# Differential attention: three query tiles transposed behind their scores, alternating with the next head's scores; bias copies in two lots

## The chip, the cores and the metric

One core of one Trainium2 chip. The metric is device time in microseconds of one execution; the kernel is run several times and the median is given. A core has a tensor engine (PE) with a weight loader (PEld), a vector engine (DVE), a scalar engine (ACT), GpSimd (POOL) and a queue that issues the DMAs here (SP). PE writes its products to PSUM, eight banks of 128 x 512 fp32; DVE and ACT read them there.

## The reference

A two-layer encoder on two sequences of 512 and 256 tokens (768 together), width 1024. Cut to what matters here:

```python
# layer 0
h = x @ w_in                                   # u | v | q | k | v_attn
out_a = gelu(u) * (W_s[g] @ layer_norm(gelu(v)) + b[g])
s = q_row @ k_win + rpb[:, row_off][:, :, col_off]   # 8 heads x 64, neighbourhood window
out_b = softmax(s) @ v_win
x = layer_norm(ALPHA * x + concat(out_a, out_b) @ w_out)
x = layer_norm(ALPHA * x + square(relu(x @ w1)) @ w2)
# layer 1: differential attention, 8 heads, two maps of 64, values of 128
s = q @ k - slope[h] * abs(q_pos - k_pos)      # both maps
p = softmax(s)
o = (p[0] - lam * p[1]) @ v
x = layer_norm(ALPHA * x + (rms_norm(o, g) * (1 - lam_init)) @ w_out)
x = layer_norm(ALPHA * x + square(relu(x @ w1)) @ w2)
```

## The kernel before

**Numbers.** Every fp32 operand of a product is split into a high part (rounded to the PE's fp32r form, on ACT: `xh`, `wh`, a "CAST") and a low part (the rest, a subtraction on DVE: `xl`, `wl`, a "TENSOR_TENSOR"). `mm3` issues three matmuls for each product: high x high, high x low, low x high (L128, L129, L130). So every weight that comes in by DMA (`raw`) passes ACT and DVE before PE can use it (`weights`, L137 on), and every PSUM result that becomes an operand passes `split` (L132).

**Tiles and stages.** The 768 tokens are six query tiles of 128: t = 0 to 3 are the long sequence, t = 4 and 5 the short one. Names of tiles end in the stage: V is the first projection (the gate's v, six PSUM banks at once, eight steps of k), U the gate's u and the first head's q and k, N0 to N7 the neighbourhood heads, O0 the output projection, F and G the MLP, D0 to D7 the differential heads of layer 1, O1 its output projection, then F and G again.

**What sets the order.** PE and SP run in the order in which the code is written. DVE, ACT and POOL are ordered by the framework's scheduler, which goes by readiness and by priorities (`high_priority`). PSUM has two groups of banks: five "pa" (scores, transposes, value products) and three "ps" (projections). A tile of a group can be written only after the last reader of the tile that held its bank is done, and banks are handed out in turn.

**Stage V and what follows.** For k = 0 the first weight comes in two halves; `between=ask` puts the two DMAs of x (columns 0 to 383, 384 to 767) behind the first half on SP, and the splits of the weight halves and of the two column spans stand behind them in the code. Before the data is there PE runs nine matmuls of ones (`warm(9)`). After V's last matmul, stand in the code: `na_copies` (twelve DMAs on SP that lay the positional bias out in DRAM scratch: eight of 8x16x512, four of 8x32x512; no other stage touches them before a head's `na_load` reads them back), the weight loads of the first three jobs (`per[:3]`: q0, k0, u0, u1), gate vectors, the spatial weights `wsb` and `bsb`, the next weight (u2), the gate's gelu and norm (`gate_norm`: gelu L191, squares L195, norms L198 and L199) with the DMAs that lay the gated rows out in chunk order (`vc`), `warm(14)` (28 matmuls in the profile), and then stage U. `gate_norm` reads V's six PSUM banks: four "pa" and two "ps".

**Heads.** `attention` makes three lists for a head: S (scores of tile t, two half scores of 128x512 for t < 4 in layer 1, then a softmax on DVE and ACT: a fused add, minimum and accumulate L339, exp L341, reciprocal L342, the combination of the two maps L1278 and L1279), T (four PE transposes of 128x128 of a tile's p, L373, then `split` into `pt` or, for t = 4 and 5 with two transposes, into `sp`), and V (value products of the long sequence from `pt`, then of the short one from `sp`). `pipeline` strings the heads together: with lag 2 a head is S0 S1, then T4 T5 and V of the head before (`carry`), then S2 T0 S3 T1 S4 T2 S5 T3. `weave` puts the fill matmuls (projections of the next head, output projection) between them by their costs; of the first `held` items only twelve fill items may stand between. In layer 1 the RMS norm of the head before (`pend`) is run at t == 2.

In the last neighbourhood head the four second-half weights of O0 (`last`, `wo0[4..7]`) are loaded, cast on ACT and subtracted on DVE.

Of the kernel before, what the change touches and what calls it, by code (L numbers as in the profile page):

```python
# [72 lines left out]
class Trunk:  # L73
# [44 lines left out]
    def stat(self, w=1):  # L118
        return self.small.tile([P, w], F32, tag=f"st{w}", name=self.uid("st"), bufs={1: 24, 2: 4, 6: 4}[w])

# [15 lines left out]
    def weights(self, src, pool=None, spare=False, parts=1, between=None):  # L136

        nc = self.nc
        raw = self.wpool.tile([P, D], F32, tag="raw", name=self.uid("raw"), bufs=3)
        if pool is None:  # L140
            hi, lo = [self.wpool.tile([P, D], F32R, tag="w", name=self.uid(n), bufs=8) for n in ("wh", "wl")]
        else:
            hi, lo = [pool.tile([P, D], F32R, tag="w2", name=self.uid(n)) for n in ("wh", "wl")]
        for i in range(parts):
            cs = slice(i * D // parts, (i + 1) * D // parts)
            nc.sync.dma_start(raw[:, cs], src[:, cs])
            if between and i == 0:
                between()
            nc.scalar.copy(hi[:, cs], raw[:, cs])
            (nc.gpsimd if spare else nc.vector).tensor_tensor(lo[:, cs], raw[:, cs], hi[:, cs].bitcast(F32), op=ALU.subtract)  # L150
        return hi, lo
# [199 lines left out]
    def attention(self, pl, prob, values, emit):  # L351
# [12 lines left out]
        def tr(t):  # L364
            def f():
# [8 lines left out]
                if t >= 4 or not self.near:  # L374
                    c = self.tok(t - base)
                    if t < 4:
                        hi, lo = [x.rearrange("p (k c) -> p k c", c=NP) for x in (hi, lo)]
                    with self.tc.high_priority(200):
                        self.split(ps[:, :n * P].rearrange("p (k c) -> p k c", c=P), hi[:, k0:k0 + n, c], lo[:, k0:k0 + n, c])
                    return  # L380

                steps = [offs[k0 + j] + (t - q0[k0 + j]) * P for j in range(n)]
                for i, (lo_j, hi_j) in enumerate(self.runs(steps)):
                    d = steps[lo_j + 1] - steps[lo_j] if hi_j - lo_j > 1 else P
                    src = ps[:, lo_j * P:hi_j * P].rearrange("p (k c) -> p k c", c=P)
                    dst = [bass.AP(tensor=x.tensor, offset=x.offset + steps[lo_j],
                                   ap=[list(x.ap[0]), [d, hi_j - lo_j], [1, P]]) for x in (hi, lo)]
                    with self.tc.high_priority(200):
                        self.split(src, dst[0], dst[1])
            return f  # L390
# [127 lines left out]
    def pipeline(self, mains, fills, wait, lag=2):  # L518


        carry = []
        for u, (S, T, V) in enumerate(mains):
            main = S[:lag] + carry
            held = len(main)
            for t in range(lag, TT):
                main += [S[t], T[t - lag]]
            carry = T[TT - lag:] + V
            if u == len(mains) - 1:
                main += [(wait, fn) for _, fn in T[TT - lag:]]
                carry = V  # L530
            weave(main, fills[u], held, 12, 1.08 if self.near else 1.04, (1500 if self.near else 3600) if u else 0,
                  lambda fn: self.scored >= getattr(fn, "after", 0))
        run(carry)

# [23 lines left out]
    def mix0(self, ahead):  # L558
# [29 lines left out]
        def mixed(g, sample):  # L588
# [7 lines left out]
            for j in range(n):  # L596
# [12 lines left out]
                [vjob(1)], [qjob(3), kjob(3)], [(oA[0], oA[1][:6])], [(oA[0], oA[1][6:])]]  # L609
        last = self.lazy(lambda: [self.weights(a["wo0"][4 + j]) for j in range(4)])  # L610
        fills = self.fillers(per)
        self.ph = "V"
        self.near, self.first, self.count, self.pw = True, (0, 0, 1, 2), (2, 3, 3, 2), 512
        self.warm(9)
        vps = [self.bank("pa" if t < 4 else "ps") for t in range(TT)]
        for k in range(NK):
            if k == 3:
                scratch, stores = self.na_rows(pl)
            if k == 6:
                for dst, src in stores:  # L620
                    nc.sync.dma_start(dst, src)
            xr = pl.tile([P, NT], F32, tag="h", name=self.uid("xr"))
            def ask():
                for c, d in SPANS if k == 0 else [(0, NT)]:
                    nc.sync.dma_start(xr[:, c:d], a["xt"][k][:, c:d])
            if k:
                ask()
            if k % 2 == 0:
                ws = self.weights(a["wv0"][k // 2], parts=1 if k else 2, between=None if k else ask)
            for c, d in SPANS:  # L630
                self.split(xr[:, c:d], self.xH[:, k, c:d], self.xL[:, k, c:d])
            wh, wl = [w[:, (k % 2) * 512:(k % 2) * 512 + 512] for w in ws]
            for t in range(TT):
                cs = self.tok(t)
                self.mm3(vps[t], self.xH[:, k, cs], self.xL[:, k, cs], wh, wl, k == 0, k == NK - 1)
        self.na_copies(scratch)
        self.key_lows(pl)
        for js in per[:3]:
            for ws, _ in js:
                ws()  # L640
        gates = pl.tile([P, 3, 512], F32, tag="h", name="gates")
        gg, gb = gates[:, 0, :], gates[:, 1, :]
# [5 lines left out]
        for ws, _ in per[3]:  # L648
            ws()
        vg, vc = [[pl.tile([P, 3, 512], F32, tag="h", name=f"{n}{h}") for h in range(2)] for n in ("vg", "vc")]  # L650
        gated = self.gate_norm(vps, [vg[i // 3][:, i % 3, :] for i in range(TT)],
# [11 lines left out]
        self.raws = [self.na_load(pl, tables, h) for h in range(1)]  # L663
        self.warm(14)
        self.ph = "U"
# [119 lines left out]

    def na_copies(self, scratch):


        for s in range(2):
            w, rows, rl = BLK[s], ROWS[s], ROWLEN[s]  # L790
            base, sc, step = scratch[s]
            for r in range(rows):
                self.nc.sync.dma_start(
                    bass.AP(tensor=sc.tensor, offset=sc.offset + r * w * step,
                            ap=[[P * step + w, NHEAD], [step + 1, w], [1, rows * rl]]),
                    bass.AP(tensor=base.tensor, offset=base.offset + (rows - 1 - r) * rl,
                            ap=[[RPB_ROWS[s] * rl, NHEAD], [0, w], [1, rows * rl]]))

# [449 lines left out]
    def mix1(self, ahead):  # L1248
# [5 lines left out]
        def unit(h):  # L1254
            self.cost_s, self.cost_r, self.cost_x, self.cost_t = 1300, 0.68, 0, 176

            def prob(t):
# [5 lines left out]
                w, c0 = c * P, 384 - P * t if t < 4 else 1024 - P * (t - 4)  # L1263
                if t == 2:
                    while pend:
# [70 lines left out]
        left = self.side("m1l", "left", dict(h=8))  # L1336
        right = self.side("m1r", "right", dict(v=2, p=6, pt=2, sp=2, tb=1, kl=1))
        pl = self.both(left, right)
# [11 lines left out]
        self.after_norm(lead)  # L1350
        self.pipeline([unit(h) for h in range(8)], fills, 2535)
        while pend:
# [116 lines left out]
```

## Time and profile before

| what | value |
|---|---|
| median of 3 runs | 1692.05 us (1691.17 to 1694.19) |
| the profiled execution, own time | 1689.46 us |
| its span in the profile | 1687.7 us |
| mean granted PE clock | 0.991 |
| DMA | 210.93 MB, mean 125 GB/s |
| first transposes of stage N wait (116.14 us) | 2.07 us for ACT's softmax |

A row of a timeline gives start, duration, engine, line, operation, written tile <- read tiles, shapes, count, and in brackets how long the engine was idle before it and who released it. A row of groups gives the line, engine, operation and count, then busy us and mean ns, then the idle time before. The granted clock is the share of full speed that PE had; 0.50 is half.

### The profile page before, as it was taken

Reading aid. Unit: us, or ns where it says so; the run is one execution under the profiler, and the core shown is the slowest. Engines: PE = TensorE matmul, PEld = TensorE weight load, DVE = VectorE, ACT = ScalarE, POOL = GpSimd, SP = SyncE. Lnnn points to the kernel's source line nnn. Section 1 sums busy time; section 2 is a strip of 40 time slices with the busy share of each in tenths; the row PEclk is TensorE's granted clock in tenths of the full one; section 3 lists DMA queues with packets and bytes.
Section 4 is the critical chain, followed back from the end, with each engine's and each line's share of the span. In section 5 each row is a group of like instructions: output and inputs, shape, how many; then the busy total and the mean of one; then the engine's idle time right before and its main releaser. Section 6 shows DMA issues by size and latency. Waiting matters only on the chain.

```text
span 1687.7 us, 23443 instructions
## 1 busy us (share of the span) xinstructions
PE 1633.7 (97%) x8926; PEld 1479.3 (88%) x8926; DVE 1226.9 (73%) x2117; ACT 933.7 (55%) x1698; POOL 45.5 (3%) x44
## 2 busy tenths in 40 slices
PE   8999998999999999999999999998999999999998
PEld 7889986899999888888988898886899999788886
DVE  3648778986766786887667676687987665786876
ACT  3546775466555544452667576775465566544442
POOL 0100000100000000001100000001100000000001
PEclk9999999999999999999999999999999999999999
DMA  7622212154355745461110111111154444745441
GB/s 246 207 96 69 69 57 76 51 198 149 140 174 186 266 141 176 145 206 61 51 50 26 50 51 38 38 38 50 51 198 173 174 167 150 265 143 183 149 165 75
DMA packets 113521, 210.93 MB, mean 125 GB/s; under 512 B 19824, under 2 KB 74352, under 8 KB 113408
## 3 DMA queue, kind: packets, MB, share of 16 engines
q1 hardware_dynamic: 113408, 209.43, 36.6%
q8 instruction: 70, 1.15, 0.3%
q14 instruction: 43, 0.35, 0.1%
HBM read 162.95 MB, written 49.08 MB: 126 GB/s over the span
## 4 chain that ended last, share of the span: by engine, by line
PE 73%; ACT 10%; DVE 9%; DMA 4%; issue 2%; SPq 1%; POOL 0%; DVEq 0%; POOLq 0%; ACTq 0%
PE psG L130 5%; PE psG L129 5%; PE psG L128 5%; PE psD L128 4%; PE psD L129 4%; PE psD L130 4%; PE psF L128 3%; PE psF L129 3%; PE psF L130 3%; PE paG L130 3%; PE paG L128 3%; PE paG L129 3%; PE paF L130 3%; PE paF L128 3%; PE paF L129 3%; DMA rwF<-in_ff_dram 2%
## 5 line engine op out<-in xcount | busy, mean ns | idle before, releaser
L128 PE MATMUL psG<-whG,hqG 128*128 128x512 f32 x336 | 131.4, 391 | 3.7 <-ACT hqG L133 3.7
L130 PE MATMUL psG<-whG,hqG 128*128 128x512 f32 x336 | 131.6, 392 | 0.5 <-DVE hqG L134 0.5
L129 PE MATMUL psG<-wlG,hqG 128*128 128x512 f32 x336 | 131.2, 391 | 0.0
L134 DVE TENSOR_TENSOR wlF<-rwF,whF 128x1024 fp32r<-128x1024 f32 x82 | 100.2, 1223 | 36.1 <-PE psF L129 31.3
L133 ACT CAST whF<-rwF 128x1024 fp32r<-128x1024 f32 (+1 forms) x110 | 102.8, 936 | 25.0 <-PE psF L129 23.2
L130 PE MATMUL paF<-xh,wlF 128*128 128x384 f32 x344 | 115.7, 336 | 0.0
L128 PE MATMUL paF<-xh,whF 128*128 128x384 f32 x344 | 115.4, 336 | 0.0
L129 PE MATMUL paF<-xl,whF 128*128 128x384 f32 x344 | 115.3, 335 | 0.0
L134 DVE TENSOR_TENSOR hqG<-hiG,hqG 128x768 fp32r<-128x768 f32 x106 | 100.4, 952 | 14.4 <-ACT hqG L133 14.4
L133 ACT CAST hqG<-hiG 128x768 fp32r<-128x768 f32 x106 | 87.6, 832 | 34.7 <-PE psG L130 17.9
L128 PE MATMUL psF<-xhO,whF 128*128 128x384 f32 x312 | 105.8, 339 | 0.6 <-DVE ctF L1047 0.4
L129 PE MATMUL psF<-xlO,whF 128*128 128x384 f32 x312 | 105.0, 337 | 0.0
L130 PE MATMUL psF<-xhO,wlF 128*128 128x384 f32 x312 | 104.8, 336 | 0.0
L128 PE MATMUL paG<-whG,hqG 128*128 128x512 f32 x252 | 98.0, 389 | 0.0
L129 PE MATMUL paG<-wlG,hqG 128*128 128x512 f32 x252 | 98.0, 389 | 0.0
L130 PE MATMUL paG<-whG,hqG 128*128 128x512 f32 x252 | 98.0, 389 | 0.0
L128 PE MATMUL psD<-xh,whD 128*128 128x384 f32 (+1 forms) x280 | 92.1, 329 | 0.0
L129 PE MATMUL psD<-xl,whD 128*128 128x384 f32 (+1 forms) x280 | 90.0, 322 | 0.0
L130 PE MATMUL psD<-xh,wlD 128*128 128x384 f32 (+1 forms) x280 | 90.0, 321 | 0.0
L341 ACT ACTIVATE pD<-pD,stD 128x512 f32<-128x512 f32 (+1 forms) x96 | 62.3, 649 | 32.4 <-DVE stD L339 32.2
L128 PEld LDWEIGHTS psG<-whG,hqG 128*128 128x128 f32 x336 | 63.5, 189 | 17.4 <-ACT hqG L133 4.3
L1005 ACT ACTIVATE ctF<-ctF 128x384 f32<-128x384 f32 x64 | 33.7, 526 | 81.2 <-DVE ctF L1047 80.6
(430 smaller groups left out, 4841.4 us busy)
## 6 DMA issues: line engine op xcount, KB each, us to landing
hiG<-hd SPq DMA_DIRECT2D x106, 384.0 KB
hd<-hsF SPq DMA_DIRECT2D x24, 1344.0 KB
rwF<-in_ff_dram SPq DMA_DIRECT2D x28, 1024.0 KB
gzG<-in_ff_dram SPq DMA_DIRECT2D x28, 512.0 KB
rawD<-in_wf_dram SPq DMA_DIRECT2D x16, 512.0 KB
rawG<-in_ff_dram SPq DMA_DIRECT2D x14, 512.0 KB
gyG<-in_ff_dram SPq DMA_DIRECT2D x14, 512.0 KB
hd<-hsO SPq DMA_DIRECT2D x4, 1344.0 KB
```

Source lines behind the costliest of these rows:

```text
L128: mm(ps, lh, rh, start=start, stop=False, **kw)
L129: mm(ps, lh, rl, start=False, stop=False, **kw)
L130: mm(ps, ll, rh, start=False, stop=stop, **kw)
L133: self.nc.scalar.copy(hi, src)
L134: self.nc.vector.tensor_sub(lo, src, hi.bitcast(F32))
L341: nc.scalar.activation(p, p, AF.Exp, bias=mn, scale=-1.0, accum_out=sm)
L1005: nc.scalar.activation(x, src, AF.Relu)
```

## The change

- `pipeline` gets a lag of 3 in layer 1: a head begins S0 T3' S1 T4' S2 T5' (the primes are tiles of the head before), then V of the head before, then S3 T0 S4 T1 S5 T2. The last head ends with three transposes. In layer 0 the lag stays 2. The RMS norm is run at t == 3, and there are seven buffers p for six.
- The first half of a weight is cast and subtracted ahead of `between`, and for k = 0 `ask` splits the first column span right after its DMAs.
- The splits of the transposes lose their priority in layer 0.
- O0's second-half weights are subtracted on POOL (`spare=True`).
- `warm(9)` becomes `warm(8)`, and `warm(14)` is gone.
- The bias copies stand in two lots on SP: eight behind the first four weight loads, four behind the fifth.
- One-wide statistics have 20 buffers for 24.

```diff
-        return self.small.tile([P, w], F32, tag=f"st{w}", name=self.uid("st"), bufs={1: 24, 2: 4, 6: 4}[w])
+        return self.small.tile([P, w], F32, tag=f"st{w}", name=self.uid("st"), bufs=20)
...
             nc.sync.dma_start(raw[:, cs], src[:, cs])
+            nc.scalar.copy(hi[:, cs], raw[:, cs])
+            (nc.gpsimd if spare else nc.vector).tensor_tensor(lo[:, cs], raw[:, cs], hi[:, cs].bitcast(F32), op=ALU.subtract)
             if between and i == 0:
                 between()
-            nc.scalar.copy(hi[:, cs], raw[:, cs])
-            (nc.gpsimd if spare else nc.vector).tensor_tensor(lo[:, cs], raw[:, cs], hi[:, cs].bitcast(F32), op=ALU.subtract)
...
-                    with self.tc.high_priority(200):
+                    with self.tc.high_priority(0 if self.near else 200):
                         self.split(ps[:, :n * P].rearrange("p (k c) -> p k c", c=P), hi[:, k0:k0 + n, c], lo[:, k0:k0 + n, c])
...
-                    with self.tc.high_priority(200):
-                        self.split(src, dst[0], dst[1])
+                    self.split(src, dst[0], dst[1])
...
     def pipeline(self, mains, fills, wait, lag=2):
-        carry = []
-        for u, (S, T, V) in enumerate(mains):
-            main = S[:lag] + carry
+        carry, V = [], []
+        for u, (S, T, V1) in enumerate(mains):
+            main = (flat(*zip(S, carry)) if lag > 2 and carry else S[:lag] + carry) + V
+            V = V1
             held = len(main)
             for t in range(lag, TT):
                 main += [S[t], T[t - lag]]
-            carry = T[TT - lag:] + V
+            carry = T[TT - lag:]
             if u == len(mains) - 1:
                 main += [(wait, fn) for _, fn in T[TT - lag:]]
-                carry = V
...
-        run(carry)
+        run(V)
...
-        last = self.lazy(lambda: [self.weights(a["wo0"][4 + j]) for j in range(4)])
+        last = self.lazy(lambda: [self.weights(a["wo0"][4 + j], spare=True) for j in range(4)])
...
-        self.warm(9)
+        self.warm(8)
...
+                if k == 0:
+                    c, d = SPANS[0]
+                    self.split(xr[:, c:d], self.xH[:, 0, c:d], self.xL[:, 0, c:d])
...
-            for c, d in SPANS:
+            for c, d in SPANS[k == 0:]:
                 self.split(xr[:, c:d], self.xH[:, k, c:d], self.xL[:, k, c:d])
...
-        self.na_copies(scratch)
         self.key_lows(pl)
         for js in per[:3]:
             for ws, _ in js:
                 ws()
+        self.na_copies(scratch, 0)
...
         for ws, _ in per[3]:
             ws()
+        self.na_copies(scratch, 1)
...
-        self.warm(14)
...
-                if t == 2:
+                if t == 3:
                     while pend:
                         pend.pop(0)()
...
-        right = self.side("m1r", "right", dict(v=2, p=6, pt=2, sp=2, tb=1, kl=1))
+        right = self.side("m1r", "right", dict(v=2, p=7, pt=2, sp=2, tb=1, kl=1))
...
-        self.pipeline([unit(h) for h in range(8)], fills, 2535)
+        self.pipeline([unit(h) for h in range(8)], fills, 2535, 3)
```

`na_copies` takes the lot `s` as an argument and does one of its two loops; its DMAs are the same.

PE at the seam from head 6 to head 7 of stage D, before: four half scores of the new head (two matmuls each), the transposes of tiles 4 and 5 of the old one, then its first value product.

```order
L1271 MATMUL paD_2075_11053<-qkD_2057_10952,qkD_1967_10523 128x512
L1272 MATMUL paD_2075_11053<-klD_7486,qkD_1967_10523 128x512
L1271 MATMUL paD_2076_11054<-qkD_2057_10952,qkD_1967_10523 128x512
L1272 MATMUL paD_2076_11054<-klD_7486,qkD_1967_10523 128x512
L1271 MATMUL paD_2086_11077<-qkD_2057_10952,qkD_1967_10523 128x512
L1272 MATMUL paD_2086_11077<-klD_7486,qkD_1967_10523 128x512
L1271 MATMUL paD_2087_11078<-qkD_2057_10952,qkD_1967_10523 128x512
L1272 MATMUL paD_2087_11078<-klD_7486,qkD_1967_10523 128x512
L373 MATMUL paD_2097_11101<-ident,pD_2048_10922 128x128 x2
L373 MATMUL paD_2098_11106<-ident,pD_2062_10985 128x128 x2
L128 MATMUL paD_2099_11111<-ptD_2021_10808,vD_2001_10647 128x512
```

The same place with the change (line numbers are one higher there): the four transposes of the old head's tile 3 stand behind the first score tile, those of tile 4 behind the second, and a third score tile follows.

```order
L1272 MATMUL paD_2073_11030<-qkD_2055_10929,qkD_1965_10500 128x512
L1273 MATMUL paD_2073_11030<-klD_7470,qkD_1965_10500 128x512
L1272 MATMUL paD_2074_11031<-qkD_2055_10929,qkD_1965_10500 128x512
L1273 MATMUL paD_2074_11031<-klD_7470,qkD_1965_10500 128x512
L373 MATMUL paD_2084_11054<-ident,pD_2022_10812 128x128 x4
L1272 MATMUL paD_2085_11061<-qkD_2055_10929,qkD_1965_10500 128x512
L1273 MATMUL paD_2085_11061<-klD_7470,qkD_1965_10500 128x512
L1272 MATMUL paD_2086_11062<-qkD_2055_10929,qkD_1965_10500 128x512
L1273 MATMUL paD_2086_11062<-klD_7470,qkD_1965_10500 128x512
L373 MATMUL paD_2096_11085<-ident,pD_2046_10899 128x128 x2
L1272 MATMUL paD_2097_11090<-qkD_2055_10929,qkD_1965_10500 128x512
L1273 MATMUL paD_2097_11090<-klD_7470,qkD_1965_10500 128x512
```

The first value product, which stood as the eleventh row, now stands behind six half scores and three transposed tiles.

SP between stages V and U, before: all twelve bias copies (`rpbs`) ahead of the weight loads (`in_wf`).

```order
L793 DMA rpbs_213<-rpbp_212 8x16x512 x8
L793 DMA rpbs_219<-rpbp_218 8x32x512 x4
L146 DMA rawV_369<-in_wf_dram 128x1024
L146 DMA rawV_375<-in_wf_dram 128x1024
L146 DMA rawV_381<-in_wf_dram 128x1024
L146 DMA rawV_387<-in_wf_dram 128x1024
L170 DMA gates<-in_gate_g_dram 128x512
```

The same place with the change, to the second lot:

```order
L146 DMA rawV_356<-in_wf_dram 128x1024
L146 DMA rawV_362<-in_wf_dram 128x1024
L146 DMA rawV_368<-in_wf_dram 128x1024
L146 DMA rawV_374<-in_wf_dram 128x1024
L794 DMA rpbs_212<-rpbp_211 8x16x512 x8
L170 DMA gates<-in_gate_g_dram 128x512
L170 DMA gates<-in_gate_b_dram 128x512
L648 DMA wsb<-in_wsp_dram 128x1024
L170 DMA bsb<-in_bsp_dram 128x1024
L146 DMA rawV_395<-in_wf_dram 128x1024
L794 DMA rpbs_218<-rpbp_217 8x32x512 x4
```

The four weight loads have moved ahead of the copies, and the last four copies behind the fifth weight load.

DVE at the start, before: both halves of the first weight's low part (`wl`), then the low parts of x (`xl`).

```order
L150 TENSOR_TENSOR wlV_121<-rawV_119,whV_120 128x512 x2
L134 TENSOR_TENSOR xl<-xrV_118,xh 128x384 x2
L134 TENSOR_TENSOR xl<-xrV_152,xh 128x384 x2
L134 TENSOR_TENSOR xl<-xrV_176,xh 128x384 x2
L150 TENSOR_TENSOR wlV_180<-rawV_178,whV_179 128x1024
```

The same place with the change:

```order
L148 TENSOR_TENSOR wlV_120<-rawV_118,whV_119 128x512
L134 TENSOR_TENSOR xl<-xrV_117,xh 128x384
L148 TENSOR_TENSOR wlV_120<-rawV_118,whV_119 128x512
L134 TENSOR_TENSOR xl<-xrV_117,xh 128x384
L134 TENSOR_TENSOR xl<-xrV_151,xh 128x384 x2
```

The first span of x now stands ahead of the second half of the weight.

More of the change, by code (lines that the diff above doesn't have):

```diff
@@ L784, in na_masks, with na_copies @@
         return masks
[L786 to L797, printed above, removed]
+    def na_copies(self, scratch, s):
+        w, rows, rl = BLK[s], ROWS[s], ROWLEN[s]
+        base, sc, step = scratch[s]
+        for r in range(rows):
+            self.nc.sync.dma_start(
+                bass.AP(tensor=sc.tensor, offset=sc.offset + r * w * step,
+                        ap=[[P * step + w, NHEAD], [step + 1, w], [1, rows * rl]]),
+                bass.AP(tensor=base.tensor, offset=base.offset + (rows - 1 - r) * rl,
+                        ap=[[RPB_ROWS[s] * rl, NHEAD], [0, w], [1, rows * rl]]))
     def na_load(self, pl, tables, h):
```

## The prediction, made before the changed kernel was run

> **What bounds the kernel now.** I read the page first, then the list of what the tensor engine (PE) waits for, then stretches of its timeline around those waits, with the granted clock.
>
> ```profile
> PE 1633.7 (97%) x8926; PEld 1479.3 (88%) x8926; DVE 1226.9 (73%) x2117; ACT 933.7 (55%) x1698; POOL 45.5 (3%) x44
> PE 73%; ACT 10%; DVE 9%; DMA 4%; issue 2%; SPq 1%; POOL 0%; DVEq 0%; POOLq 0%; ACTq 0%
> ```
>
> PE is busy 97% of the span and carries most of the last chain, so nothing but PE's pauses, its slow-clock stretches and matmuls without use can be won: the span less PE's busy time is 54 us, and only part of it lies where the diff works.
>
> ```profile
> PE paN L373 <- ACT pN L715: 9.2, 9, 2.1
> PE paD L373 <- ACT pD L1279: 4.5, 6, 1.4
> PE paD L128 <- DVE stD L339: 4.2, 4, 1.3
> PE paD L373 <- DVE stD L339: 3.1, 3, 1.9
> PE paD L128 <- DVE spD L134: 1.9, 2, 1.3
> ```
>
> Columns: the waiting instruction, its releaser, us in total, times, longest. The last three rows are the seams between heads of stage D: 4.2 + 3.1 + 1.9 = 9.2 us.
>
> ```profile
> 7.50:14.20 6.70, 5.09 (x12) 4.03 (x13) 5.37 (x11) 5.42 (x11) 0.00 (x0) 0.50 0.97 376
> 871.00:874.40 3.40, 3.07 (x7) 2.48 (x8) 2.88 (x11) 1.96 (x6) 0.00 (x0) 0.50 0.00 0
> 903.50:907.00 3.50, 2.72 (x15) 2.09 (x13) 2.89 (x10) 1.97 (x7) 0.00 (x0) 1.00 0.00 0
> 953.00:956.30 3.30, 3.30 (x10) 2.56 (x8) 2.42 (x8) 1.43 (x3) 0.00 (x0) 0.50 0.00 0
> 1045.20:1048.50 3.30, 3.26 (x8) 2.59 (x9) 2.65 (x9) 1.55 (x5) 0.00 (x0) 0.50 0.07 30
> ```
>
> These are stretches with their length, then PE, weight loads, DVE, ACT and POOL, then the granted clock. Three D seams ran at half clock right after their pauses, as did the start; the seam at 903 us did not. Each such stretch of 3.4 us does 1.7 us of work: 1.7 us lost.
>
> **The change part by part.**
>
> *Start (V).* The order lists show the low half of the first 384 columns subtracted between the two weight halves, not after both.
>
> ```profile
> 4.56 0.69 DVE L150 TENSOR_TENSOR wlV<-rawV,whV 128x512 fp32r<-128x512 f32 x1 [1.61 <-ACT whV L149]
> 7.76 0.51 ACT L133 CAST xh<-xrV 128x384 fp32r<-128x384 f32 x1
> 8.50 3.12 DVE L134 TENSOR_TENSOR xl<-xrV,xh 128x384 fp32r<-128x384 f32 x6
> 9.11 0.79 PE L130 MATMUL paV<-whV,xl 128*128 128x512 f32 x1 [3.30 <-DVE xl L134]
> 43.98 0.39 PE L128 MATMUL psV<-whV,xh 128*128 128x512 f32 x1
> 44.68 3.29 PE L116 MATMUL paV<-ones 128*128 128x128 f32 x28
> ```
>
> The first subtraction ends at 5.25, one xl span takes 3.12/6 = 0.52, so PE's third matmul can go at 5.8 instead of 9.11. Three query tiles (9 matmuls) are fed by that span; the tenth needs the other half (xh at 8.27, xl near 9.1). So at 9.1 nine more matmuls are done. The stage's last three take 44.68 - 43.98 = 0.70 at full clock, 0.233 each. If the stretch to 14.2 stays at half clock, the gain at the end of the stage is 9 x 0.233 = 2.1. If it runs at full clock, as the shorter pauses (0.4 before 5.8, then about 1 before 9.1) let me think, the 5.1 us from 9.1 hold 22 matmuls instead of 11, eleven more, x 0.233 = 2.6 on top: 4.7. I take **4.0**, nearer to the upper end; range 2.1 to 4.7. Eight warm-up matmuls instead of nine cost nothing, as PE waits for data behind them.
>
> *From V to the gates (U).* Out go 14 warm-up calls (28 matmuls), 44.68 to 47.72 where the first projection starts: 3.0 us.
>
> ```profile
> 44.23 1.05 ACT L149 CAST whV<-rawV 128x1024 fp32r<-128x1024 f32 x1 [23.12 <-DMA rawV<-in_wf_dram]
> 47.80 1.28 ACT L191 ACT_TABLE_LOAD   x1
> 52.34 0.61 ACT L191 ACTIVATE vg<-psV 128x512 f32<-128x512 f32 x1
> 53.10 0.44 PE L128 MATMUL psU<-xh,whV 128*128 128x384 f32 x1 [0.97 <-ACT vg L191]
> 62.15 0.41 PE L128 MATMUL psU<-xh,whV 128*128 128x384 f32 x1 [0.46 <-DVE qkU L446]
> 16.11 14.68 SPq L793 DMA_DIRECT2D rpbs<-rpbp  x12
> ```
>
> The second projection span needs a PSUM bank that the fifth gelu frees (53.10, 8.4 us behind V's end). ACT waited 23.12 us for a weight load that stood behind the twelve bias copies on SP's queue; now four loads stand ahead of them, so three casts run inside V and only the fourth (u1, whose buffer V's last matmul frees) comes after. Then: 1.05 + 1.28 + five gelus at 0.6 = 5.4 us behind V's end, where PE's first span has ended 4.3 behind it (62.15 - 0.46 - 53.10 = 8.6 for two spans): a wait of 1.1, and 3.0 us saved. The fourth span needs the first one's evacuation, which now stands in ACT's order behind four squares, a cast and two more squares: by estimate 15.5 us behind V's end, against 62.15 - 44.68 = 17.5 before. So **2.0** are left, and two pauses of 1.1 and about 1.5 us lie close together without the warm-ups: a half-clock stretch there would take 1.7 back. I take 1.0, range -1 to 3. The first weight loads leave the queue 9.8 us of issue time earlier (eight copies of 14.68/12 = 1.22). The last four copies (4.9 us of queue) now stand behind the fifth weight load, ahead of the vc loads; their data is wanted first by stage N's first head, and the vc loads wait for gelu and norm anyway. Nothing is charged; if that cover went, the mixing matmuls would be up to 4.9 us late.
>
> *Stage N.* Four subtractions of 128x1024 go from DVE to POOL, and the splits lose their priority; PE's order is the same there.
>
> ```profile
> L150 DVE TENSOR_TENSOR wlN<-rawN,whN 128x1024 fp32r<-128x1024 f32 x16 | 19.6, 1222 | 4.2 <-ACT whN L149 4.2
> 254.79 0.44 PE L373 MATMUL paN<-ident,pN 128*128 128x128 f32 x2 [1.43 <-ACT pN L715]
> L470 POOL MEMSET klD<- 64x768 f32 x2 | 1.5, 736 | 0.1
> masks.py:199 POOL TENSOR_SCALAR_AFFINE_SELECT ident<-ident 128x128 f32<-128x128 f32 x1 | 0.3, 294 | 0.1
> ```
>
> DVE is spared 4 x 1.22 = 4.9 us, two of them in the last head, where PE paused for 1.43 twice. What an elementwise subtraction costs POOL no row shows: between 0.98 us (the memset by width, 736 x 1024/768) and 2.35 (the select, 294 x 8). At 2.35 the last two low halves are ready just as the output projection asks for them; at 4 it would stall some 3 us. I take 2.35, the op with an input, no stall. The lost priority can move a split behind a cast of 1.05 or in front of it. Together I take **1.0**, range -3 to 3. The Trainium skill, GPSIMD Engine Reference, 3.1 (Elementwise), measures 4497 ns on GpSimd against 2293 on VectorE for one elementwise op; scaled by half, an estimate of 2.25 us, which would leave the sum alone.
>
> *D seams.* Before, PE did two score tiles, then T4, T5 and V of the head before. Now S0 T3 S1 T4 S2 T5, then V.
>
> ```profile
> 867.32 0.39 PE L1271 MATMUL paD<-qkD,qkD 128*128 128x512 f32 x1
> 868.25 0.38 PE L373 MATMUL paD<-ident,pD 128*128 128x128 f32 x2
> 869.56 0.44 PE L373 MATMUL paD<-ident,pD 128*128 128x128 f32 x2 [0.93 <-DVE stD L339]
> 871.33 0.79 PE L128 MATMUL paD<-ptD,vD 128*128 128x512 f32 x1 [1.34 <-DVE stD L339]
> 904.72 0.50 PE L128 MATMUL paD<-ptD,vD 128*128 128x512 f32 x1 [0.78 <-DVE stD L339]
> 952.12 0.50 PE L128 MATMUL paD<-ptD,vD 128*128 128x512 f32 x1 [1.34 <-DVE stD L339]
> 1044.19 0.44 PE L373 MATMUL paD<-ident,pD 128*128 128x128 f32 x2 [1.87 <-DVE stD L339]
> 1045.24 0.80 PE L128 MATMUL paD<-ptD,vD 128*128 128x512 f32 x1 [0.61 <-DVE spD L134]
> 950.35 0.44 PE L373 MATMUL paD<-ident,pD 128*128 128x128 f32 x2 [0.31 <-DVE stD L339]
> 949.59 0.69 DVE L339 CUSTOM_DVE_ANT_0 pD<-paD,al 128x512 f32<-128x512 f32 x1
> 951.37 0.69 DVE L339 CUSTOM_DVE_ANT_0 pD<-paD,al 128x512 f32<-128x512 f32 x1
> ```
>
> One score tile is 868.25 - 867.32 = 0.93 us of PE; DVE takes a half score each 951.37 - 949.59 = 1.78 us (reduction, ACT's exp, reciprocal). Five "pa" banks hold four half scores and T4; T5 needs the bank of the first half, V that of the second, both freed by L339. That is the wait. Now a transpose of ready data and a third score tile, with the fill matmuls woven after the first items, stand between a score and the bank it must give back. I walked one seam with these steps: S0 to 0.93, T3, fill, S1 to 3.4, T4, S2 to 5.1, T5 waits for the third half score (5.75) 0.65, V for T4's split 0.2: about 0.85 left, in pieces below those that brought half clock. Seven seams at 0.8 are 5.6; before, 9.2 of waits and three half-clock stretches of 1.7 are 14.3. Gain **8.7**; at worst the waits merely move (0), at best all go (14.3). The pending RMS work runs one tile later and one more p buffer covers the third live tile; both hide under V and the fills, and cost a wait of one L339 (0.69) if that cover goes.
>
> *Last head.*
>
> ```profile
> 1140.97 0.66 PE L373 MATMUL paD<-ident,pD 128*128 128x128 f32 x4 [0.96 <-ACT pD L1279]
> 1144.92 0.66 PE L373 MATMUL paD<-ident,pD 128*128 128x128 f32 x4 [1.43 <-ACT pD L1279]
> ```
>
> T(t-2) waits for its softmax; with T(t-3) the tile has one more score's time. Of the row's 4.5 us over six waits, I take **2.5** gone (0 to 4); the last tile's chain remains.
>
> Sum: 4.0 + 1.0 + 1.0 + 8.7 + 2.5 = 17.2. The profiled execution took 1689.46 (span 1687.7, the rest around it), so it would take 1672.3. It lies 2.6 under the median of 1692.05; off that, 1674.9, and I say **1675**.
>
> **The rivals.**
>
> - *The half clock stays at the seams.* Then 3 x 1.7 = 5.1 fall out: 1692.05 - 12.1 = **1680**. Against it: the seam at 903 us, with a single wait of 0.78, kept full clock; those at 871, 953 and 1045, with 0.93 + 1.34, 0.31 + 1.34 and 1.87 + 0.61, did not. The Trainium skill, TensorE: Matmul & The Clock Gate, Part 1, lets the clock fall after a whole idle window of about 3.4 us; by that these short pauses would not be the cause and the loss would stay. The trace speaks against it: half clock at 953 behind 1.65 us of pauses.
> - *DVE sets the seam.* Three score tiles ask DVE for six half scores, 10.7 us, and PE waits as long as before for banks: the 8.7 fall out, **1683.5**. For it: the 1.78 us step is unchanged. Against: T3, T4 and the fill matmuls now stand between the scores, so PE asks for the banks later.
> - *Slower.* If T5 and V wait 2.5 us in all at each of seven seams, and each pause brings half clock, seams cost 7 x (2.5 + 1.7) = 29.4 against 14.3: 15.1 lost instead of 8.7 won, 17.2 - 23.8 = -6.6: **1698.7**. It decides when the remaining pause of a seam passes about 1.65 us, the 1.34 + 0.31 above; my walk says 0.85.
> - *The U stage gives all back*, or POOL needs 4 us a subtraction: 3 less, **1678**; inside the forecast's spread.
> - *More*: seams free of waits and the lower DVE load in N worth 3: **1664**.
>
> **How the numbers follow.** Forecast (1669 to 1680, the U and POOL cases in it) 0.53; half clock stays 0.13; DVE sets the seam 0.16; more 0.10; slower 0.04; no net change, as a mix of several losses, 0.04. The range, 1664 to 1687, takes in all but the last two and the best part of "more". A measurement of this kernel tells 0.2%, 3.4 us, from no change: faster 0.92, same 0.04, slower 0.04.
>
> **What would show it.** V: the third matmul before 6 us, full clock between 7.5 and 14, V's end near 40.5. U: no ones matmul there, second span about 5.4 us behind V's end, no half-clock stretch to 65. N: POOL subtractions at 2.4 us or less and no wait at stage O's first matmuls. D: seam waits on L339 well under 6 us in all and no granted clock of 0.50 at a seam; last head's transpose waits near 2. The prediction is wrong if the seams' waits change their name (splits, L1279) and keep their length, or if waits grow in N, where only the scheduler's order moved.

## The result, and the profile after

The changed kernel takes 1677.51 us (median of 6 runs, 1675.50 to 1679.89), the kernel before 1691.61 (6 runs, 1684.22 to 1694.19): a ratio of 0.9939, 95% interval 0.9922 to 0.9955. That is 14.1 us, 0.8%, off the medians; the profiled executions, 1689.46 and 1676.29, are 13.2 apart. Forecast were 1675 and 17.2 us. One of the five executions of the last experiment ran at a mean granted clock of 0.556 and took 2708.07 us; its figures below are of the other four.

The total agrees better than its parts. In the page of the changed kernel PE has lost 9.3 us of busy time, and its share of the last chain has risen from 73 to 80%:

```profile
PE 1624.4 (97%) x8896; PEld 1472.7 (88%) x8896; DVE 1227.0 (73%) x2113; ACT 934.0 (56%) x1698; POOL 54.9 (3%) x48
PE 80%; ACT 8%; DVE 8%; issue 3%; POOL 1%; DMA 1%; DVEq 0%; POOLq 0%; ACTq 0%; SPq 0%
```

Where the time went shows in the starts of the stages' first matmuls in the two traces (V's first row is the start of V's first matmul; U's is the first projection):

| stage | starts before | after | stage longer or shorter by |
|---|---|---|---|
| V, with the warm-ups behind it | 5.00 | 5.01 | -9.0 |
| U | 47.72 | 38.73 | **+9.1** |
| N | 104.66 | 104.78 | -2.5 |
| O0, F, G of layer 0 | 275.70 | 273.31 | -2.5 |
| D | 765.48 | 760.57 | -7.3 |
| O1 and the rest | 1156.95 | 1144.70 | -0.9 |

All that the start and the missing warm-ups won was lost again inside stage U. The list of PE's waits (waiting instruction, releaser, us in total, times, longest) names the place in its first row, which has no counterpart of that size before:

```profile
PE psU L128 <- DVE qkU L445: 7.3, 1, 7.3
PE paN L373 <- ACT pN L717: 5.1, 5, 1.4
...
PE paD L373 <- ACT pD L1280: 3.0, 3, 1.4
PE paD L128 <- DVE stD L339: 2.5, 4, 1.0
PE paN L403 <- DVE ptN L134: 2.5, 3, 1.6
...
PE paD L1272 <- DVE stD L339: 1.9, 4, 0.7
...
PE psO L129 <- POOL wlN L148: 1.1, 1, 1.1
...
PE psD L128 <- DVE nat L266: 0.8, 1, 0.8
PE paD L373 <- DVE stD L339: 0.7, 2, 0.4
```

The timeline of the changed kernel at that place, with DVE, ACT, POOL and PE:

```profile
50.89 0.84 ACT L441 ACTIVATE qkU<-psU 64x384 fp32r<-64x384 f32 x2
...
56.47 0.91 POOL L181 TENSOR_TENSOR stV<-stV,half 128x1 f32<-128x1 f32 x1 [0.71 <-DVE stV L180]
57.42 0.75 DVE L199 SCALAR_TENSOR_TENSOR vg<-vg,stV,gates 128x512 f32<-128x512 f32 x1 [0.44 <-POOL stV L181]
58.20 1.66 DVE L445 SCALAR_TENSOR_TENSOR qkU<-psU,qkU 64x384 fp32r<-64x384 f32 x3
...
60.01 0.66 PE L128 MATMUL psU<-xh,whV 128*128 128x384 f32 x1 [7.31 <-DVE qkU L445]
```

ACT had begun its half of q's evacuation at 50.89. DVE's half (L445) stood behind all six gate norms, each of which goes to POOL for a power and back, and came at 58.20. PE's fourth projection span needs the bank that it frees. In the kernel before, q's first evacuations (L446 there) had stood among the norms on DVE, ahead of two of the L198:

```profile
60.21 1.02 DVE L446 SCALAR_TENSOR_TENSOR qkU<-psU,qkU 64x384 fp32r<-64x384 f32 x2
...
63.24 1.41 DVE L198 SCALAR_TENSOR_TENSOR vg<-vg,stV,gates 128x512 f32<-128x512 f32 x2
```

The granted clock (length, PE, weight loads, DVE, ACT, POOL, clock, DMA share, GB/s) at the places shown of before, and at the new slow ones:

```profile
7.50:14.20 6.70, 6.70 (x29) 5.22 (x29) 5.33 (x12) 5.30 (x10) 0.00 (x0) 1.00 0.95 367
...
57.00:63.80 6.80, 3.79 (x12) 3.82 (x13) 4.00 (x7) 2.30 (x5) 0.38 (x1) 0.50 0.31 82
254.90:258.30 3.40, 3.40 (x10) 2.67 (x9) 2.44 (x8) 1.40 (x4) 0.00 (x0) 0.51 0.23 93
871.00:874.40 3.40, 3.40 (x21) 3.40 (x20) 2.04 (x8) 3.40 (x9) 0.00 (x0) 1.00 0.01 2
...
1045.20:1048.50 3.30, 3.30 (x18) 2.77 (x17) 2.40 (x4) 1.80 (x4) 0.00 (x0) 1.00 0.16 30
```

The start runs at full clock now, and so do the seams of stage D. Half clock has come to U, from the 7.31 us pause on; the stretch at 254.9 in stage N stands against one at 116.7 before.

### The profile page after: what moved, and what is told of

It is laid out like the page before. It is cut to its first block, busy times and chain, and to the rows that moved or that the text cites. A ratio compares the mean times of both kernels' runs of the same rounds, so it can differ in the third digit from the quotient of the medians.

```text
span 1674.5 us, 23392 instructions
## 1 busy us (share of the span) xinstructions
PE 1624.4 (97%) x8896; PEld 1472.7 (88%) x8896; DVE 1227.0 (73%) x2113; ACT 934.0 (56%) x1698; POOL 54.9 (3%) x48
## 4 chain that ended last, share of the span: by engine, by line
PE 80%; ACT 8%; DVE 8%; issue 3%; POOL 1%; DMA 1%; DVEq 0%; POOLq 0%; ACTq 0%; SPq 0%
PE psG L130 5%; PE psG L128 5%; PE psG L129 5%; PE psF L129 4%; PE psF L128 4%; PE psF L130 4%; PE paF L130 4%; PE paF L129 4%; PE paF L128 4%; PE psD L128 3%; PE psD L129 3%; PE psD L130 3%; PE paG L128 3%; PE paG L130 3%; PE paG L129 3%
## 5 line engine op out<-in xcount | busy, mean ns | idle before, releaser
L134 DVE TENSOR_TENSOR hqG<-hiG,hqG 128x768 fp32r<-128x768 f32 x106 | 100.4, 952 | 15.5 <-ACT hqG L133 15.5
L128 PEld LDWEIGHTS psG<-whG,hqG 128*128 128x128 f32 x336 | 63.5, 189 | 17.5 <-ACT hqG L133 4.3
L130 PEld LDWEIGHTS psG<-whG,hqG 128*128 128x128 f32 x336 | 63.5, 189 | 14.7 <-DVE hqG L134 1.4
```

The source lines that it names most:

```text
L128: mm(ps, lh, rh, start=start, stop=False, **kw)
L130: mm(ps, ll, rh, start=False, stop=stop, **kw)
L134: self.nc.vector.tensor_sub(lo, src, hi.bitcast(F32))
```

## The experiments

Eleven runs. Ratios are to the kernel before on the same chip; kernels measured on different chips are compared through their ratios. Four kernels were built on the changed kernel, one on the kernel before, and the others on the second experiment's kernel, in which stage U is mended, so that what they change is not covered by its wait.

**e1: the alternation undone.**

```diff
-        self.pipeline([unit(h) for h in range(8)], fills, 2535, 3)
+        self.pipeline([unit(h) for h in range(8)], fills, 2535)
-                if t == 3:
+                if t == 2:
```

> The changed kernel with the alternation undone: stage D strings its heads as before (lag 2, RMS at the third score tile). My theory: the seam alternation is what won the 7.3 us between the start and the end of stage D (391.5 us before, 384.1 changed), three half-clock stretches included; so this kernel takes 5 to 10 us more than the changed one, about 1685, its D seams wait 8 us or more on L339 again, and one to three half-clock stretches come back between 850 and 1130 us. Rival: stage D shortened because it began at another phase of the clock window, or because of more p buffers; then the time stays within 2 us of the changed kernel's 1677.5 and half clock stays away.

1682.15 us, ratio 0.9956 (0.9942 to 0.9970). Stage D (first row: length and PE's busy time, clock at the end) and a stretch of it, then D's waits:

```profile
1040.40:1043.70 3.30, 3.30 (x9) 2.52 (x9) 2.45 (x8) 2.10 (x5) 0.00 (x0) 0.50 0.00 0
762.80:1151.44 388.64, 374.26 (x2282) 339.10 (x2280) 275.34 (x672) 251.87 (x539) 11.82 (x10) 1.00 0.13 43
```

```profile
PE paD L373 <- ACT pD L1280: 4.5, 6, 1.4
PE paD L128 <- DVE stD L339: 4.3, 4, 1.4
PE paD L373 <- DVE stD L339: 2.7, 2, 1.7
PE paD L128 <- DVE spD L134: 1.9, 2, 1.3
```

Stage D is 388.6 us long against 384.1 (1144.70 - 760.57): 4.5 longer, just under the lower end of what I expected, and the time is on the low side too. One half-clock stretch came back, where the kernel before had three. The waits of the kernel before are nearly all there again, so the theory holds for the waits. For the clock the rival has a share, as the same seam shows in the two kernels:

```profile
866.37 0.44 PE L373 MATMUL paD<-ident,pD 128*128 128x128 f32 x2 [0.93 <-DVE stD L339]
868.14 0.50 PE L128 MATMUL paD<-ptD,vD 128*128 128x512 f32 x1 [1.34 <-DVE stD L339]
```

In e1 the first seam waits 0.93 and 1.34 us, to the hundredth what it waited before at 869.56 and 871.33, and this time no half clock followed; the last section says what differs. Without the clock (1.7 us a stretch) D is 388.6 - 1.7 = 386.9 here and 391.5 - 5.1 = 386.4 before, against 384.1: the alternation saves 2.3 to 2.8 us, and half clock besides. The saving is not the waits alone. PE's listed waits in D add up to 14.8 us before, 14.1 in e1 and 9.6 with the change, which is 4.5 to 5.2 less. PE's busy time in D is 376.5, 374.3 and 374.0 us, and with 1.7 taken off for each slow stretch 371.4, 372.6 and 374.0: by this estimate PE's own work takes 1.4 to 2.6 us longer in the alternating order, which gives a part back. Which matmuls take longer is not shown here.

The half clock of D goes with the alternation. The ten traces with the alternation (the changed kernel, e2 to e8, e10 and e11) have a stage D of 383.9 to 384.3 us and no half-clock stretch in it; the three without have three (before), one (e1) and two (e9).

**e2: the first head's projections ahead of the gate norms.** The code of stage U's first fill jobs moves ahead of the norms L198 and L199; PE's order is the same.

```diff
             rs.append(self.power(sq, 1.0 / 512))
+        yield
         for x, mean, r in zip(xs, means, rs):
...
+        next(gated)
+        with self.tc.high_priority(200):
+            run(fills[0])
         for i, _ in enumerate(gated):
...
         self.ph = "U"
-        with self.tc.high_priority(200):
-            run(fills[0])
```

> The changed kernel, with the first head's projections written ahead of the gate norms, so that DVE has the q evacuations (L445, L446 here) ahead of or among the norms L198 and L199; nothing else differs. My theory: the 7.31 us wait of PE in stage U came from DVE's order, six gate norms with their round trips to POOL ahead of the evacuation, and it also brought the half-clock stretch of 6.83 us. Then that wait falls under 2 us, the half clock at 57 us goes, and the time is 1667 to 1674. Rival: the DMAs set the end of the stage (the vc loads land near 70 us whatever DVE does): then PE waits at the first mixing matmuls instead, and the time stays within 3 us of 1677.5.

1668.94 us, ratio 0.9881 (0.9861 to 0.9901): 8.6 us under the changed kernel's median, about 10 by the ratios. In its timeline, DVE first, then PE, then the stretch of U's half clock, q's first evacuations (L446 here, at 43.87 and 45.53 us; their tiles are named V) stand ahead of every norm, and PE waits 1.4 us for a gelu, as forecast, and then for nothing until the mixing matmuls (L598), where a wait of 0.66 and one of 0.27 are left:

```profile
43.87 0.55 DVE L446 SCALAR_TENSOR_TENSOR qkV<-psV,qkV 64x384 fp32r<-64x384 f32 x1 [0.20 <-ACT qkV L442]
...
46.42 0.75 DVE L199 SCALAR_TENSOR_TENSOR vg<-vg,stV,gates 128x512 f32<-128x512 f32 x1
```

```profile
65.47 1.05 PE L598 MATMUL paU<-wsb,vc 128*128 128x128 f32 x8
67.18 0.46 PE L598 MATMUL paU<-wsb,vc 128*128 128x128 f32 x2 [0.66 <-issue]
67.91 0.46 PE L598 MATMUL paU<-wsb,vc 128*128 128x128 f32 x2 [0.27 <-DMA vc<-vg]
```

```profile
57.00:63.80 6.80, 6.80 (x36) 5.71 (x35) 4.23 (x7) 3.49 (x8) 0.91 (x1) 1.00 0.38 92
```

The half clock at 57 us is gone, and stage N starts at 97.22 and not at 104.78. DVE's order and the half clock behind it cost the changed kernel 7.6 us; the rival, that the vc loads set the end, falls.

**e3: besides, the second lot of copies behind the vc loads.**

```diff
-        self.na_copies(scratch, 1)
         vg, vc = ...
...
+        self.na_copies(scratch, 1)
         for ws, _ in per[4]:
             ws()
```

> As the kernel with the projections ahead of the norms, and besides, the second lot of bias copies (four DMAs of 512 KB) stands behind the vc loads on SP, not ahead of them. If the copies hold up the vc loads (20.4 us of issue in the changed kernel against 15.2 before), the vc loads land some 5 us earlier and this kernel is 2 to 6 us faster than the one with the projections ahead alone. If the vc loads only follow the norms, the two are within 1.5 us.

1675.16 us, ratio 0.9913 (0.9895 to 0.9930): slower than e2, which neither case expected. The vc loads left the queue by 61.3 us and not by 66.0, yet the mixing matmuls began at 65.37 against e2's 65.47: the vc loads had nothing to win. PE now waits for the cast of the next weight, and half clock follows at 90.9. The cast in e2, then in e3, then the wait:

```profile
70.57 1.04 ACT L147 CAST whV<-rawV 128x1024 fp32r<-128x1024 f32 x1
```

```profile
88.78 1.04 ACT L147 CAST whV<-rawV 128x1024 fp32r<-128x1024 f32 x1
```

```profile
PE psU L128 <- ACT whV L147: 3.6, 1, 3.6
```

That weight's DMA left SP no later than in e2 (64.35 us against 66.12). Its cast came 18 us later, in ACT's order behind two more rounds of u's evacuations. So here too an edit of SP's queue moved another engine's order. How far the copies also held up the weight's landing is not shown.

**e4: the copies in one place**, ahead of the weight loads, as before.

```diff
-        self.na_copies(scratch, 0)
...
-        self.na_copies(scratch, 1)
...
+        self.na_copies(scratch, 0)
+        self.na_copies(scratch, 1)
         self.key_lows(pl)
```

> The changed kernel with all twelve bias copies in one place ahead of the weight loads, as before. In the order of DVE this alone puts the evacuations back among the norms. My theory: the first projections then wait for their weights (landing near 44 us, V ends near 38.7), some 6 us, but the 7.3 us wait behind DVE is gone, so stage N starts at 102 to 105 us and the time is within 3 us of the changed kernel's: the two lots won nothing in the end. Rival: two lots are worth what the earlier weights give, 5 us or more; then this kernel takes 1682 or more.

1678.10 us, ratio 0.9932 (0.9911 to 0.9954): the same as the changed kernel. PE:

```profile
44.93 0.69 PE L128 MATMUL psU<-xh,whV 128*128 128x384 f32 x1 [5.76 <-ACT whV L147]
...
61.87 0.41 PE L128 MATMUL psU<-xh,whV 128*128 128x384 f32 x1 [0.45 <-DVE qkU L445]
```

The 7.31 us wait behind DVE is 0.45, and a wait of 5.76 for the first weight stands in its place, with half clock from 42.9 us for 6.83; stage N starts at 104.91. The two lots bring the weights early, but the scheduler's order of DVE changes with them, and in the changed kernel the one is paid for by the other.

**e5: the alternation alone, on the kernel before** (the new `pipeline`, lag 3, RMS at t == 3, seven p buffers, 20 statistics buffers).

> The kernel before with the alternation alone (lag 3 in layer 1, RMS at the fourth score tile, seven p buffers). My theory: stage D loses 4 to 5 us of waits, as the undo of the same part showed, and up to three half-clock stretches of 1.7 us where their phase lets them go: stage D takes 383 to 387 us against 391.5, and the time is 0.3 to 0.5% under the kernel before. Rival: the seam's gain depends on the earlier stages' shift alone; then the time is within 2 us of the kernel before.

1682.30 us, ratio 0.9958 (0.9942 to 0.9973). Stage D in the trace, one stretch with the same columns as above:

```profile
767.55:1151.62 384.07, 374.00 (x2281) 336.67 (x2280) 275.32 (x672) 250.25 (x539) 11.82 (x10) 1.00 0.14 44
```

384.07 us, within 0.1 of the changed kernel's, at another place in time: the stage's length is the alternation's and not the earlier stages'. The rival falls.

**e6: the output projection's low halves on DVE**, on e2 (`spare=True` taken out).

> The kernel with the projections ahead of the gate norms, with the four low halves of the output projection's weights subtracted on DVE again and not on POOL. If POOL's subtractions won in stage N what DVE's four (4.9 us) cost before, stage N is 1 to 3 us longer here and the last head's transposes wait more on L717's softmax; if POOL only moved the wait to stage O's first matmuls (1.1 us there), the time is within 1.5 us of 1668.9.

1671.22 us, ratio 0.9889 (0.9866 to 0.9913), not told apart from e2 by time. Stage N is 170.4 us long (267.06 - 96.66) against e2's 168.6 (265.83 - 97.22), 1.8 more, with one half-clock stretch in each. The transposes' waits on the softmax, which were to grow, did not (5.1 us against 5.2). One wait accounts for the difference, of a value product on a split that stands on DVE behind two of the subtractions:

```profile
263.86 2.35 DVE L148 TENSOR_TENSOR wlN<-rawN,whN 128x1024 fp32r<-128x1024 f32 x2
266.13 0.42 DVE L134 TENSOR_TENSOR spN<-paN,spN 128x256 fp32r<-128x256 f32 x1
```

```profile
266.60 0.39 PE L405 MATMUL paN<-spN,vN 128*128 128x256 f32 x1 [1.87 <-DVE spN L134]
```

POOL was worth that much in the stage, and from there to stage D nothing is given back (487.2 us against 487.3). The traces still end 0.7 us apart the other way: e6 began N 0.6 earlier and has no half clock at 1425 us, where e2 has a stretch of 3.41.

**e7: the splits at priority 200 again**, on e2.

> The kernel with the projections ahead of the gate norms, with the transposes' splits at priority 200 again in stage N. In the changed kernel the value products of stage N waited 2.5 us on these splits (L134), which they did not before, while the transposes waited 4 us less on the softmax. My theory: the priority is what moved the one into the other; here the waits on ptN go, those on the softmax rise to 7 or more, and the time is 0 to 3 us above 1668.9. Rival: the priority changes nothing in time (within 1 us).

1673.45 us, ratio 0.9907 (0.9881 to 0.9934): 4.5 us above e2's median, where 0 to 3 were expected.

```profile
PE paN L374 <- ACT pN L720: 8.9, 8, 2.4
```

In its list the wait on `ptN` is gone and that on the softmax is 8.9 us, as expected. Stage N is 172.1 us long (270.11 - 98.02), 3.5 more than e2's; it had 6.83 us of half clock to e2's 3.41, which makes 1.7 of these. The intervals of the two ratios overlap, so the traces carry this, not the times.

**e8: the warm-ups back**, on the changed kernel.

> The changed kernel with the fourteen warm-up calls between stages V and U again (28 matmuls, 3 us of PE). My theory: in the changed kernel what sets the end of the fourth projection span is the chain of gelu, square, POOL and DVE that begins at V's end, so three more us of PE before it are covered: the wait of 7.31 us falls to about 4.3, and the time is within 1.5 us of 1677.5; taking the warm-ups out won nothing. If the pauses then are short enough to keep full clock, it may be up to 3 us faster. Rival: the warm-ups cost their 3 us, 1680.5.

1679.41 us, ratio 0.9937 (0.9913 to 0.9961): no change.

```profile
59.95 0.66 PE L128 MATMUL psU<-xh,whV 128*128 128x384 f32 x1 [5.51 <-DVE qkU L445]
```

The fourth span starts at 59.95 with the warm-ups and at 60.01 without. The wait is 5.51 and not the 4.3 expected, since PE's wait of 1.0 us for a gelu is gone too. Taking them out won nothing here.

**e9: lag 3 without the alternation**, on e2.

```diff
-            main = (flat(*zip(S, carry)) if lag > 2 and carry else S[:lag] + carry) + V
+            main = S[:lag] + carry + V
```

> The kernel with the projections ahead of the gate norms, with lag 3 in stage D but without the alternation: S0 S1 S2, then T3 T4 T5 and V of the head before. My theory: the banks are given back at DVE's pace of one half score in 1.78 us, so the sixth half score and the transposes behind it wait for it with nothing of PE's in between; each seam waits 1.5 to 3 us more, some bring half clock, stage D takes 392 to 405 us against 384.5, and the time is 8 to 20 us above 1668.9. Rival: it is the lag, the later transposes, that won, and the alternation adds nothing: within 2 us of 1668.9.

1681.07 us, ratio 0.9956 (0.9942 to 0.9970), 12 us over e2. Stage D, one of its two half-clock stretches, and its waits at the seams:

```profile
753.97:1149.46 395.49, 378.70 (x2281) 339.56 (x2280) 275.35 (x672) 250.50 (x539) 10.88 (x10) 0.99 0.13 42
```

```profile
942.30:945.70 3.40, 3.40 (x9) 2.61 (x8) 2.42 (x8) 1.45 (x4) 0.00 (x0) 0.51 0.02 5
```

```profile
PE paD L374 <- DVE stD L340: 7.0, 10, 1.3
PE paD L374 <- ACT spD L133: 2.6, 2, 1.3
...
PE paD L374 <- DVE ptD L134: 2.1, 4, 0.8
```

395.5 us against 384.2: behind three score tiles in a row, the transposes (L374) wait for the banks that DVE and ACT give back at their pace. The order of the pieces wins, not the longer lag; the lag alone makes the stage worse than it was (391.5 us, with three half-clock stretches).

**e10: the start as before**, on e2 (both spans of x split behind both weight halves).

> The kernel with the projections ahead of the gate norms, with the start as before: both weight halves cast and subtracted ahead of both column spans of x. My theory: PE's first low-half matmul waits 2 to 3.3 us again and V ends 4 to 6 us later than 38.7 (43.5 to 44.7, by whether the first stretch falls to half clock); nothing behind it takes that up, so the time is 3.5 to 6 us above 1668.9. Rival: stage U's chain of gelus and DMAs covers it; then within 1.5 us.

1670.82 us, ratio 0.9899 (0.9883 to 0.9915).

```profile
8.63 0.59 PE L130 MATMUL paV<-whV,xl 128*128 128x512 f32 x1 [2.70 <-DVE xl L134]
```

The wait of 2.70 us is back, one half-clock stretch follows it (8.9 us, 3.41 long), V ends at 42.83, 4.1 us later than e2's, and stage N starts 2.8 us later (100.01 against 97.22). The time is 1.9 above e2's and 1.1 above e11's, the same kernel on the same chip as e10, where 3.5 to 6 were expected; by the time alone the rival, within 1.5, is not excluded. The traces say why: the distance is still 2.9 us at the start of stage D, and in O1 and behind it e2 and e11 have a half-clock stretch (3.41 us at 1425) that e10 has not.

**e11: e2 once more**, five rounds.

> The kernel with the projections ahead of the gate norms once more, in five rounds against the kernel before, since it is the fastest so far: a ratio of 0.986 to 0.990.

1669.73 us (median of four, 1668.64 to 1671.27), ratio 0.9891 (0.9875 to 0.9908), within what was expected. It beats both kernels: its interval and the changed kernel's (0.9922 to 0.9955) do not meet.

## Why the prediction was right, and where it was not

The total was right (17.2 forecast, 14.1 measured, 13.2 between the traces), but that is in part luck. V and U together fell 5 us short and stage D 3.9, while N gave 1.5 more than forecast and stages outside the sum 3.4.

*Start: right.* The third matmul, the first to use a low half of x, ran at 5.92 us, and the clock stayed full. V ended at 38.73, 5.95 us earlier than before (44.68); 4.0 were forecast. Not all of it is the change: the second weight half's cast started at 7.24 us before and at 6.29 after, and e5, with the old start, ended V at 43.5 (its warm-ups begin there). That cast's start moves between runs of the same order (6.77 us in e10). e10 puts the early span alone at 4.1 us of V's end, close to the 4.0, and at 2.8 by stage N.

*Stage U: wrong.* The step that failed is "by estimate 15.5 us behind V's end" for the fourth span: it came at 60.01 - 38.73 = 21.3. I had walked ACT's order and left out DVE's. The evacuation has two halves, and the one on DVE stood behind six norms. In place of the 2.0 us that this step was to save the runs showed a wait of 7.31 us and half clock behind it: V with its warm-ups and U together forecast 5.0, measured 0. e2 wins 7.6 of this back by order alone, e8 shows that the warm-ups' 3 us were covered by it, and e4 that it came with the new places of the copies, for which I had charged nothing. My rival "the U stage gives all back" was priced at 3 and was worth 5. A remark of the same passage misread the queue, though the sum does not use it: all twelve copies had stood ahead of the first weight loads, not eight, so those left 15.8 us earlier (15.14 against 30.90) and not 9.8.

*Stage N: right sign, under-sized.* 2.5 us against 1.0. The traces of e6 and e7 put 1.8 on POOL's subtractions and 1.8 on the priority; together that is more than the 2.5, so the two do not simply add. POOL's price was close (2.35 taken):

```profile
L148 POOL TENSOR_TENSOR wlN<-rawN,whN 128x1024 fp32r<-128x1024 f32 x4 | 9.7, 2440 | 209.7 <-DVE nat L268 190.8 <-ACT whN L147 18.9
```

At 2.44 us each, the last of them came 1.1 us late for stage O's eleventh matmul, where I had said no stall: POOL began the second pair at 272.03, 1.3 us ahead of stage O. In e2 it began 2.8 ahead (262.99 against 265.83), and that wait is gone.

*D seams and last head: right mechanism, over-sized.* Forecast 8.7 + 2.5, measured 7.3. The seam's waits came to the size walked: 2.5 + 1.9 + 0.7 and one of 0.2 are 5.3 us, 5.6 were forecast; only they lie mostly at the value products and the score tiles, where my walk had them at T5. The last head's transposes went from 4.5 to 3.0 us, 1.5 and not 2.5. What the sum put at nothing made up the rest: waits of the projections for their banks grew from 0.2 to 1.3 us (`nat`, L266 and L268), and PE's own work in the alternating order takes 1.4 to 2.6 us more, by the estimate under e1. The half clock's 5.1 us came as forecast, in part by luck: the old order brought three stretches in one trace and one in another. The rival that half clock stays fell; that DVE sets the seam fell for the alternation and is what e9 shows without it.

*Outside the sum* O0, F and G of layer 0 lost 2.5 us and O1 and the rest 0.9. A half-clock stretch at 335 us that the changed kernel does not have is 1.7 of it; for the rest no cause is shown.

## What to carry to other kernels

An evacuation that two engines share is as late as the later of the two queues: walk both, and any helper that a queue's head waits for. Where a scheduler orders engines, an edit of one queue (here DMAs on SP) can reorder another; look at the order of every engine between the edit and the next wait, and price what stands ahead. Between a product and the bank it must give back, put work whose inputs are ready; more of the same kind in a row made the stage longer (e9).

## What the runs showed of the hardware

The half-clock stretches come in one length, 3.41 us or twice that (but for the one in which each execution ends), and in the kernel before the three of stage D start at 871.0, 952.9 and 1045.1, that is 24 and 27 such lengths apart within 0.1 us: a grid that runs by itself. The same two pauses (0.93 and 1.34 us) brought half clock before and none in e1, so where they fall on the grid counts as well as their length. The windows of this grid just ahead of the three stretches, and then e1's window at the first seam (columns as above; PE's busy time is the second number):

```profile
867.61:871.02 3.41, 1.45 (x8) 0.80 (x6) 2.99 (x7) 1.95 (x5) 0.00 (x0) 1.00 0.43 154
949.53:952.95 3.42, 1.78 (x10) 1.14 (x9) 2.82 (x9) 2.74 (x7) 0.00 (x0) 1.00 0.41 153
1041.69:1045.11 3.42, 1.07 (x6) 0.48 (x4) 3.29 (x7) 2.03 (x6) 0.00 (x0) 1.00 0.37 115
```

```profile
866.19:869.61 3.42, 1.91 (x8) 1.44 (x9) 2.82 (x11) 2.27 (x6) 0.00 (x0) 1.00 0.38 137
```

PE stood idle 1.96, 1.64 and 2.35 us ahead of half clock. In e1 the grid cuts the pause of 0.93 us in two, and the window holds 1.51. Over all 13 traces, each of the 43 full-clock windows with 1.95 us or more of idle was followed by half clock, none of the 6208 with less than 1.5 was, and of the 41 between 19 were. So it is the sum of the pauses in one window that decides, at about half of the window. The Trainium skill, TensorE: Matmul & The Clock Gate, Part 1, says that the window runs freely, and the trace agrees; it also asks for an idle window of about 3.4 us before the clock falls, and here 1.64 us in pieces were enough.

A subtraction of 128x1024 took POOL 2.44 us and DVE 1.22.
